# Where eight sums of down-projection weights stand on VectorE, and when their loads begin

## The chip, the cores and the metric

The kernel runs on 1 core of one Trainium2 chip. The metric is the device time of one execution in microseconds (us). Lower is better.

## The reference

One layer of a streaming encoder over 2048 prompt tokens and 8 x 16 sample tokens, width 1024, all in float32. What is computed, cut to the lines that matter here:

```python
qm, km, vm, om, ip, fp, qa, ka, va = split_in(x @ w_in)          # input projection
hm, C1, n1, m1 = mlstm_chunkwise(qm, km, vm, logi, logf, ...)    # matrix memory, 4 heads x 128
ha = swa_prompt(qa, ka, va, attn_sinks)                          # sliding-window attention
mix = jnp.concatenate([hm, ha], axis=-1) @ w_out
h = layer_norm(DEEPNORM_ALPHA * x + mix, ln1_g, ln1_b)
...
u = h @ w_up                                                     # 1024 -> 2 x 2816
c = b_conv + sum(ext[:, j:j + T] * w_conv[j] for j in range(3))  # causal convolution
a, g = jnp.split(c, 2, axis=-1)
f = (jax.nn.silu(g) * a) @ w_down                                # 2816 -> 1024
y = layer_norm(DEEPNORM_ALPHA * h + f, ln2_g, ln2_b)
```

## The kernel before

Every large product is made of three matmuls on halves of float32 numbers: ScalarE rounds an operand to a high half (`split`, L217, or L565 for x), VectorE subtracts to get the low half (L218, L566), and TensorE adds high x high, high x low and low x high. Over that lies a scheme of fast matrix multiplication in which a 2 x 2 block product takes seven products, numbered 1 to 7, instead of eight. It needs sums and differences of blocks of the operands, and a result block is put together from several products by VectorE and ScalarE.

The **input projection** (`i_dense`) runs over 4 blocks b of tokens and, in each, 5 groups g of output columns. Each (b, g) has the seven products. From block 1 on, their order is 1, 7, 6, 2 in group 0; then in every group 5, product 1 of the next group, 3, 4; and in the later groups 6, 7, 2 ahead of that. The last group ends 6, 7, 5, 2, 3, 4. Each product is 24 matmuls of 256 columns (L704). Three PSUM banks A, B, C hold them. After a product `i_after` empties what is due: after product 5 ScalarE copies bank B (L771) and VectorE adds bank C to it (L775 in groups 0 and 1, L777 in the later groups), after 4 VectorE adds bank C to another copy in the same way, after 2 and 3 ScalarE copies bank A and B out (L763). In group 3 the result goes through tanh on ScalarE (L760) and an addition of 1 on VectorE (L761).

Beside this, three chains of smaller work for tokens that are already projected are woven between the matmuls by a planner that works with fixed costs (`Chains.weave`): the matrix memory (among its VectorE steps bst L1150, C L1223, hn L1156, mr L1157 to L1159; ScalarE's mr L1153; TensorE's transposes pht L1176 and products pnum L1211), and the attention. The order of TensorE's instructions is the program's own order; the other engines' orders, and that of SyncE, which issues nearly all DMAs, come from a scheduler that takes the earliest instruction of the program among those it believes ready, by its own estimate of times. Each engine then executes its queue in that fixed order.

The **down projection**, much later, uses the seven products too, and for it needs differences of blocks of its weights. There are 11 pairs of rows of blocks (`NK2`). For each pair, `d_sums(k, step)` does three steps: step 0 loads two 128 x 1024 tiles x and y of weights (L844, L845, 512 KB each), step 1 makes four subtractions of 128 x 512 on VectorE (L850 to L853), step 2 stores x and y to DRAM (L855, L856). All three are called `txy` in the profile. Eight of the pairs are done in blocks 2 and 3 of the input projection, one in each of the groups 0 to 3, the other three in the output projection (`o_block`).

The buffers of the sums are those of the raw x: `xr1` to `xr4`, one for each quarter of a block of x. The next block's quarters are loaded by `x_load` (L537) after product 1 of the last group and turned into halves by `x_steps` beside the products of the last group (L547 is its first difference, of quarters 4 and 2; L550, L553, L557 the others). In the last block, `x_pair` (L892) loads operands of the output projection into the same four buffers. A sum uses `xr1` and `xr3`, so that each sum's loads wait for the store of the sum before.

Of the kernel before, what the change touches and what calls it, by code (L numbers as in the profile page):

```python
# [8 lines left out]
F32 = mybir.dt.float32  # L9
F32R = mybir.dt.float32r  # L10
AF = mybir.ActivationFunctionType
ALU = mybir.AluOpType
AX = mybir.AxisListType

P = 128
D = 1024
# [13 lines left out]
KSCALE = float(np.float32(128.0 ** -0.5))  # L30
# [174 lines left out]
class Prog:  # L205
# [381 lines left out]
    def i_dense(self):  # L587
        nc, a = self.nc, self.a
        nb = len(IBLOCKS)
        last = NG - 1  # L590

        self.next_raw()
        self.x_load(0, 2)
        for _ in range(3):
            self.next_raw()
        self.x_load(0, 4)
        self.single_raw = self.tp.tile([P, KD, P], F32, name="xsr", tag="pth", bufs=2)
        nc.sync.dma_start(self.single_raw, a["xs"])
        self.angles = {}
        self.rope_load(IBLOCKS[0][2], 2)  # L600
        self.rope_load(NPT, 1)
        self.next_split()
        self.x_steps(0, "b12")
        for _ in range(3):
            self.next_split()
        self.x_steps(0, 3)
        self.x_single(1, 2)
        self.x_load(0, 1)
        self.next_raw()
        self.x_load(0, 3)  # L610
        self.x_steps(0, 1)
        self.advance()
        self.x_steps(0, 2, "t3", 7, "t2", 6)
        self.x_single(4)
        self.x_steps(0, "t1", 5, "t4")
        self.sb, self.trans = {}, None

        passages = [{1: ["load"], 7: ["t3", 7], 6: ["t2", 6], 3: [3, "t4"], 4: ["b12", "t1"]},
                    {1: ["load"], 6: ["t3"], 7: [7, "t2"], 5: [6], 3: [3, "t4"], 4: ["b12", "t1"]}]
        sums = 0  # L620
        after = None
        for item in self.items:
            if after:

                after[0] -= 1
                if after[0] == 3:
                    self.logs_of(after[1] - 1)
                if after[0] < 0:
                    self.i_done = after[1]
                    after = None  # L630
            self.chains.hold = item[0] == "t" and item[1] > 0
            if item[0] == "t":
                _, b, ti, e = item
                if ("g", e, 3) not in self.wu:
                    self.advance()
                if b not in self.gates:
                    self.gates[b] = self.tp.tile([P, 5, 8], F32, name="gates", tag="gates", bufs=2)
                ps = self.bank([P, 512], "pg") if ti == 4 else self.ib[ti % 2 * 2]
                yield from self.i_direct(b, ti, e, ps)
                self.i_keys(b, ti, ps)  # L640
                if ti == 1:
                    if b + 1 < nb:
                        self.x_steps(b + 1, 1, 2)
                    else:
                        self.release(4)
                    after = [6, b + 1]
                elif ti == 3 and b or ti == 4:
                    self.release(4)
                    self.x_steps(b, 4)
                    if b:  # L650
                        self.x_steps(b, 5)
                self.advance()
                continue
            _, b, g, s = item
            if item not in self.wu:
                self.advance()
            yield from self.i_product(b, g, s)
            del self.wu[item]
            self.release(2)
            if self.trans and s != 4:  # L660
                self.i_transposes()
            with self.tc.high_priority():
                behind = self.i_after(b, g, s)
            if (b, g, s) == (0, 0, 7):
                self.t_setup()
            if (g, s) == (1, 6):
                self.rope_load(IBLOCKS[b][0], 2)
            if g == last and b + 1 < nb:
                if s == 7:
                    self.rope_load(IBLOCKS[b + 1][2], 2)  # L670
                for x in passages[b > 0].get(s, ()):
                    if x == "load":
                        self.spare = True
                        self.x_load(b + 1, 1, 2, 3, 4)
                    else:
                        self.x_steps(b + 1, x)
            if g == last and b + 1 == nb and s in (7, 5, 2, 3):
                self.x_pair(0, (7, 5, 2, 3).index(s))
            with self.tc.issue_after(behind) if behind and b == 0 else nullcontext():
                self.advance()  # L680

            if b >= nb // 2 and g < last:

                steps = (6, 2, 5) if g == last - 1 else (6, 5, 3)
                if s in steps:
                    self.d_sums(sums, steps.index(s))
                    sums += s == steps[2]
        self.sums = sums
        self.logs_of(nb - 1)
        self.chains.hold = False  # L690
# [64 lines left out]
    def i_out(self, b, g, i, j, src):  # L755

        nc = self.nc
        ev = src if i else self.zev()
        if g == 3:
            nc.scalar.activation(ev, src, AF.Tanh, scale=0.5)  # L760
            nc.vector.tensor_scalar_add(ev, ev, 1.0)  # L761
        elif not i:
            nc.scalar.copy(ev, src)  # L763
        if g == 2:
            self.rope(ev, IBLOCKS[b][2 * j], 2)
        self.i_store(b, g, i, j, ev)

    def i_after(self, b, g, s):
        nc, V = self.nc, self.nc.vector
        A, B, C = self.ib  # L770
        copy = lambda d, x: nc.scalar.activation(d, x, AF.Copy, scale=KSCALE) if g < 2 else nc.scalar.copy(d, x)  # L771

        def add(u):
            if g < 2:
                V.scalar_tensor_tensor(u, C, KSCALE, u, op0=ALU.mult, op1=ALU.add)  # L775
            else:
                V.tensor_add(u, C, u)  # L777
        if s == 1 and g == 0:
            return nc.scalar.copy(B, A).ins
        elif s == 6:  # L780
            self.u2 = self.zev()
            copy(self.u2, B)
        elif s == 2:
            self.i_out(b, g, 0, 0, A)
        elif s == 5:
            u4 = self.zev()
            copy(u4, B)
            add(u4)
            self.i_out(b, g, 1, 1, u4)
        elif s == 4:  # L790
            add(self.u2)
            self.i_out(b, g, 1, 0, self.u2)
            if b == 0:
                self.i_batch(g)
        elif s == 3:
            self.i_out(b, g, 0, 1, B)
            if g + 1 < NG:

                nc.scalar.copy(B, A)
# [40 lines left out]
    def d_sums(self, k, step):  # L840
        nc, V = self.nc, self.nc.vector
        if step == 0:
            self.txy = x, y = [self.xp.tile([P, D], F32, name="txy", tag=f"xr{q}", bufs=1) for q in (1, 3)]
            nc.sync.dma_start(x, self.a["wdn"][k])  # L844
            nc.sync.dma_start(y, self.a["wdn"][NK2 + k])  # L845
            return
        x, y = self.txy
        if step == 1:
            l, r = slice(0, 512), slice(512, D)
            V.tensor_sub(x[:, l], x[:, r], x[:, l])  # L850
            V.tensor_sub(x[:, r], y[:, r], x[:, r])
            V.tensor_sub(y[:, r], y[:, r], x[:, l])
            V.tensor_sub(y[:, l], y[:, l], y[:, r])  # L853
            return
        nc.sync.dma_start(self.zt[0, k], x)  # L855
        nc.sync.dma_start(self.zt[1, k], y)  # L856
# [1329 lines left out]
```

## Time and profile before

| | |
|---|---|
| median of 3 runs | 2314.28 us (2314.28 to 2319.7) |
| the profiled execution's own time | 2316.15 us |
| its span, first to last instruction | 2314.3 us |
| TensorE busy (PE) | 2281.9 us, 99% |
| VectorE busy (DVE) | 1808.1 us, 78% |
| ScalarE busy (ACT) | 1269.0 us, 55% |
| granted TensorE clock, mean | 0.996 |

PE is TensorE's matmuls, PEld its weight loads, DVE VectorE, ACT ScalarE, POOL GpSimd and SPq the queue of SyncE. In a row of a timeline stand start and length in us, engine, line, operation, what it writes and reads, and in brackets how long the engine was idle before and what ended that. Such a releaser is inferred from semaphores. The sums of blocks 2 and 3 lie between 299 and 565 us of the span.

### The profile page before, as it was taken

Reading aid. Unit: us, or ns where it says so; the run is one execution under the profiler, and the core shown is the slowest. Engines: PE = TensorE matmul, PEld = TensorE weight load, DVE = VectorE, ACT = ScalarE, POOL = GpSimd, SP = SyncE. Lnnn points to the kernel's source line nnn. Section 1 sums busy time; section 2 is a strip of 40 time slices with the busy share of each in tenths; the row PEclk is TensorE's granted clock in tenths of the full one; section 3 lists DMA queues with packets and bytes.
Section 4 is the critical chain, followed back from the end, with each engine's and each line's share of the span. In section 5 each row is a group of like instructions: output and inputs, shape, how many; then the busy total and the mean of one; then the engine's idle time right before and its main releaser. Section 6 shows DMA issues by size and latency. Waiting matters only on the chain.

```text
span 2314.3 us, 39788 instructions
## 1 busy us (share of the span) xinstructions
PE 2281.9 (99%) x14293; PEld 2094.9 (91%) x14293; DVE 1808.1 (78%) x3075; ACT 1269.0 (55%) x2377; POOL 279.5 (12%) x509
## 2 busy tenths in 40 slices
PE   8999999999999999999999999999999999999998
PEld 8999989989877778999999999999999978888876
DVE  8777687787688888998788777678766786895987
ACT  5453466776766655555656555555555544444442
POOL 0001000000011212121002000013111200100200
PEclk9999999999999999999999999999999999999999
DMA  7888999999977757888778889978898776756743
GB/s 276 287 308 297 301 309 336 314 310 342 315 269 240 240 201 270 303 319 311 276 289 274 306 304 311 315 264 287 312 294 261 225 282 208 261 175 215 255 157 108
DMA packets 300166, 632.38 MB, mean 273 GB/s; under 512 B 47869, under 2 KB 141121, under 8 KB 299969
## 3 DMA queue, kind: packets, MB, share of 16 engines
q1 hardware_dynamic: 295296, 616.14, 77.9%
q0 software_dynamic: 3520, 10.56, 1.4%
q10 hardware_dynamic: 1152, 3.15, 0.4%
q8 instruction: 113, 1.85, 0.3%
q14 instruction: 85, 0.69, 0.1%
HBM read 458.11 MB, written 171.64 MB: 272 GB/s over the span
## 4 chain that ended last, share of the span: by engine, by line
PE 76%; DVE 5%; DMA 4%; issue 2%; ACT 1%; SPq 0%; POOL 0%; DVEq 0%; ACTq 0%; POOLq 0%
PE dps L1873 19%; PE fup L1873 19%; PE dps L704 7%; PE dps L2083 6%; PE fht L2083 6%; PE fup L2083 6%; PE dps L222 2%; PE dps L224 2%; PE dps L223 2%; PE ppo L1348 1%; PE psc L1303 1%; PE ppt L1342 1%; DVE w L218 1%; PE fht L1697 1%; DMA txy<-wdn 0%
## 5 line engine op out<-in xcount | busy, mean ns | idle before, releaser
L1873 PE MATMUL dps<-hh,uw 128*128 128x384 f32 (+1 forms) x1848 | 478.7, 328 | 2.0 <-DVE u L1904 2.0
L1873 PE MATMUL fup<-hh,uw 128*128 128x384 f32 (+1 forms) x1848 | 478.2, 328 | 1.5 <-ACT ua L1894 1.5
L1873 PEld LDWEIGHTS dps<-hh,uw 128*128 128x128 f32 x1848 | 330.5, 188 | 2.2 <-DVE u L1904 2.2
L1873 PEld LDWEIGHTS fup<-hh,uw 128*128 128x128 f32 x1848 | 330.0, 188 | 2.0 <-ACT ua L1894 1.9
L1930 DVE SCALAR_TENSOR_TENSOR cc<-u,cw,cc 128x768 f32<-128x768 f32 (+1 forms) x264 | 258.1, 978 | 64.9 <-ACT cc L1928 55.5
L1873 PE MATMUL fup<-hl,uw 128*128 128x384 f32 (+1 forms) x924 | 302.5, 327 | 1.7 <-DVE hl L218 1.7
L1873 PE MATMUL dps<-hl,uw 128*128 128x384 f32 (+1 forms) x924 | 302.8, 328 | 0.0
L704 PE MATMUL dps<-w,oh 128*128 128x256 f32 x1344 | 254.3, 284 | 0.7 <-DVE zev L777 0.7
L217 ACT CAST uw<-wraw 128x1024 fp32r<-128x1024 f32 x126 | 123.0, 979 | 223.8 <-PE dps L2083 120.1
L218 DVE TENSOR_TENSOR w<-wraw,w 128x1024 fp32r<-128x1024 f32 (+2 forms) x167 | 189.4, 1141 | 56.1 <-ACT w L217 48.9
L217 ACT CAST w<-wraw 128x1024 fp32r<-128x1024 f32 (+2 forms) x167 | 163.0, 985 | 107.3 <-PE dps L704 38.9
L704 PEld LDWEIGHTS dps<-w,oh 128*128 128x128 f32 x1344 | 210.5, 188 | 11.8 <-issue 8.1
L218 DVE TENSOR_TENSOR uw<-wraw,uw 128x1024 fp32r<-128x1024 f32 x126 | 142.4, 1131 | 65.7 <-ACT uw L217 65.5
L704 PE MATMUL dps<-w,ol 128*128 128x256 f32 x672 | 187.8, 279 | 0.0
L704 PE MATMUL dps<-oh,w 128*128 128x256 f32 x896 | 170.9, 285 | 6.6 <-ACT mr L1153 3.8
L1873 PEld LDWEIGHTS fup<-hl,uw 128*128 128x128 f32 x924 | 173.5, 188 | 2.4 <-DVE hl L218 2.3
L2083 PE MATMUL fup<-uw,fu 128*128 128x512 f32 x726 | 174.2, 396 | 0.6 <-DVE uw L218 0.6
L1873 PEld LDWEIGHTS dps<-hl,uw 128*128 128x128 f32 x924 | 173.8, 188 | 0.0
L2083 PEld LDWEIGHTS fup<-uw,fu 128*128 128x128 f32 x726 | 136.6, 188 | 34.1 <-DVE uw L218 1.1
L2083 PE MATMUL dps<-uw,fu 128*128 128x512 f32 x660 | 165.3, 396 | 1.1 <-DVE uw L218 1.1
L1928 ACT ACTIVATE cc<-u,cw 128x768 f32<-128x768 f32 (+1 forms) x132 | 132.2, 1002 | 57.8 <-DVE u L1910 28.5
L704 PEld LDWEIGHTS dps<-oh,w 128*128 128x128 f32 x896 | 142.2, 191 | 13.1 <-ACT mr L1153 4.1
(318 smaller groups left out, 4567.0 us busy)
## 6 DMA issues: line engine op xcount, KB each, us to landing
uw<-zw SPq DMA_DIRECT2D x176, 512.0 KB, 5.1
zw<-uw SPq DMA_DIRECT2D x88, 512.0 KB, 3.7
w<-zws SPq DMA_DIRECT2D x72, 512.0 KB, 6.2
wv<-wup SPq DMA_DIRECT2D x66, 512.0 KB, 5.0
wraw<-wi SPq DMA_DIRECT2D x65, 512.0 KB, 5.1
wraw<-zt SPq DMA_DIRECT2D x60, 512.0 KB, 4.3
wraw<-wdn SPq DMA_DIRECT2D x45, 512.0 KB, 4.3
wraw<-wo SPq DMA_DIRECT2D x40, 512.0 KB, 4.5
```

The source lines that it names most:

```text
L217: nc.scalar.copy(hi, src)
L218: nc.vector.tensor_sub(lo, src, hi.bitcast(F32))
L222: mm(out, ah, bh, start=start, stop=False)
L223: mm(out, ah, bl, start=False, stop=False)
L224: mm(out, al, bh, start=False, stop=stop)
L704: mm(o, l, r, start=s in (1, 7) and c == k == i == 0, stop=k == 3 and i == 2, skip_group_check=True)
L1303: nc.tensor.matmul(ps[kvh][:, j, :nk], q[rs, j0 + j], k[rs, sel], start=i == 0, stop=i == 2)
L1342: nc.tensor.transpose(pp[:, j * P:(j + 1) * P], scs[j // 2][:, 2 * kvh + j % 2, kt * P:(kt + 1) * P], self.ident)
L1873: mm(ps, l[:, k], r[:, k], start=s in (1, 7) and k == 0 and i == 0, stop=k == 3 and i == 2, skip_group_check=True)
L1928: S.activation(c[:, v], u[:, 2:2 + n], AF.Identity, bias=w[3], scale=w[2])
L1930: V.scalar_tensor_tensor(c[:, v], u[:, i:i + n], w[i], c[:, v], op0=ALU.mult, op1=ALU.add)
L2083: mm(ps, l[:, k, c], r[:, k], start=s in (1, 4, 7) and u == 0 and k == 0 and i == 0, stop=u == nu - 1 and k == n - 1 and i == 2, skip_grou ...
```

## The change

Three things change in the input projection. A sum's load (step 0) moves: the first of a block is begun after product 1 of group 0, the others after product 4 of the group before; until now it was begun after product 6 of its own group. Its subtractions (step 1) are still called at product 5 (at 2 in group 3) and its stores at product 3 (at 5 in group 3), but each VectorE instruction of step 1 gets an ordering edge behind the operation that last emptied a bank, which `i_out` and `i_after` now keep in `self.emptied`: the scheduler may not put it ahead of that one in VectorE's queue. And sums use `xr1` and `xr3`, or `xr2` and `xr4`, in turn, and the next block's quarters are loaded in the order 1, 3, 2, 4.

```diff
@@ i_dense
                     if x == "load":
                         self.spare = True
-                        self.x_load(b + 1, 1, 2, 3, 4)
+                        self.x_load(b + 1, 1, 3, 2, 4)
...
-            if b >= nb // 2 and g < last:
-
-                steps = (6, 2, 5) if g == last - 1 else (6, 5, 3)
-                if s in steps:
-                    self.d_sums(sums, steps.index(s))
-                    sums += s == steps[2]
+            if b >= nb // 2:
+
+                if (g, s) == (0, 1) or s == 4 and g < last - 1:
+                    self.d_sums(sums, 0)
+                    sums += 1
+                elif g < last and s in ((2, 5) if g == last - 1 else (5, 3)):
+                    with self.tc.issue_after(self.emptied):
+                        self.d_sums(sums - 1, 2 if s == 3 or g == last - 1 and s == 5 else 1)
@@ i_out
-            nc.vector.tensor_scalar_add(ev, ev, 1.0)
+            self.emptied = nc.vector.tensor_scalar_add(ev, ev, 1.0).ins
@@ i_after
             if g < 2:
-                V.scalar_tensor_tensor(u, C, KSCALE, u, op0=ALU.mult, op1=ALU.add)
+                self.emptied = V.scalar_tensor_tensor(u, C, KSCALE, u, op0=ALU.mult, op1=ALU.add).ins
             else:
-                V.tensor_add(u, C, u)
+                self.emptied = V.tensor_add(u, C, u).ins
@@ d_sums
         if step == 0:
-            self.txy = x, y = [self.xp.tile([P, D], F32, name="txy", tag=f"xr{q}", bufs=1) for q in (1, 3)]
+            self.txy = x, y = [self.xp.tile([P, D], F32, name="txy", tag=f"xr{q}", bufs=1) for q in ((1, 3), (2, 4))[k % 2]]
```

## The prediction

> **What bounds the kernel now.** I read the page first, then the windows view over the input projection, the waits of TensorE there, and the timelines of VectorE, ScalarE, TensorE and SyncE around each wait.
>
> ```profile
> span 2314.3 us, 39788 instructions
> PE 2281.9 (99%) x14293; PEld 2094.9 (91%) x14293; DVE 1808.1 (78%) x3075; ACT 1269.0 (55%) x2377; POOL 279.5 (12%) x509
> ```
>
> TensorE is busy 99% of the span, idle 2314.3 - 2281.9 = 32.4 us in all. Its instruction order is written out by hand and the change leaves it alone, so the time moves only by TensorE waits that go or come. The change acts on eight of the eleven sums of down-projection weights, between 297 and 565 us. There the windows view (columns: stretch, its length, busy us of PE, PEld, DVE, ACT, POOL with counts, granted clock, DMA share, GB/s) gives
>
> ```profile
> 320.00:360.00 40.00, 36.13 (x294) 34.06 (x294) 30.45 (x86) 29.92 (x80) 3.00 (x6) 0.96 0.97 321
> 360.00:400.00 40.00, 40.00 (x342) 37.48 (x341) 27.29 (x87) 25.10 (x67) 3.84 (x8) 1.00 0.99 343
> 440.00:480.00 40.00, 39.72 (x337) 37.87 (x337) 37.18 (x105) 30.45 (x70) 1.26 (x3) 1.00 0.85 269
> ```
>
> One stretch loses 3.9 us of TensorE and some clock; 360 to 400, with a sum in it, loses nothing. The waits view of TensorE from 290 to 630 us names the losses (us in total, times, longest):
>
> ```profile
> PE dps L704 <- ACT mr L1153: 3.8, 1, 3.8
> PE pht L1176 <- DVE ql L218: 1.0, 1, 1.0
> PE ppo L1348 <- ACT pth L1343: 0.6, 1, 0.6
> PE pnum L1211 <- issue: 0.6, 2, 0.3
> ```
>
> None names a sum, but the timelines lead each of the first three to one. VectorE's:
>
> ```profile
> 325.20 0.69 DVE L850 TENSOR_TENSOR txy<-txy 128x512 f32<-128x512 f32 x1 [3.92 <-DMA txy<-wdn]
> 516.33 0.69 DVE L851 TENSOR_TENSOR txy<-txy 128x512 f32<-128x512 f32 x1 [4.37 <-DMA txy<-wdn]
> 539.60 0.69 DVE L850 TENSOR_TENSOR txy<-txy 128x512 f32<-128x512 f32 x1 [4.22 <-DMA zqk<-zev]
> ```
>
> VectorE works in order. Three times it stood about 4 us at a sum whose weights had not landed (the third is put down to a store of zev, but the operation reads only txy). ScalarE's timeline shows how the first stop reaches TensorE:
>
> ```profile
> 328.63 0.17 ACT L1153 ACTIVATE mr<-pnum 128x2 f32<-128x2 f32 x1 [3.17 <-DVE bst L1150]
> 329.66 0.59 ACT L771 ACTIVATE zev<-dps 128x512 f32<-128x512 f32 x1
> ```
>
> bst (L1150) stood in VectorE's queue behind the sum, ScalarE stood behind bst, and behind that stood the copy L771 that empties the bank TensorE wants.
>
> **The change part by part.** *The early sums go.* The program puts a sum's four subtractions at product 5 of its group, but the schedule pulled them forward into whatever VectorE time it thought free. Now they are tied behind the emptying operation of that product (L775 or L777, and L761 in group 3), and the loads are issued one group sooner, into two pairs of buffers. No operation is added: eight sums of four subtractions, 16 loads and 16 stores stay. A load then has about a group, some 30 us (the first group's L775 follows the copy L771 at 329.66, the next group's is the row of 357.77 below), where before it was wanted ahead of its landing, so I take all three stops as gone. Worth, from TensorE's timeline:
>
> ```profile
> 330.30 0.58 PE L704 MATMUL dps<-oh,w 128*128 128x256 f32 x1 [3.85 <-ACT mr L1153]
> ...
> 330.89 0.63 PE L704 MATMUL dps<-oh,w 128*128 128x256 f32 x2
> 331.32 0.41 PE L704 MATMUL dps<-ol,w 128*128 128x256 f32 x1
> 331.53 0.63 PE L704 MATMUL dps<-oh,w 128*128 128x256 f32 x2
> ...
> 333.24 0.29 PE L704 MATMUL dps<-ol,w 128*128 128x256 f32 x1
> 333.37 0.40 PE L704 MATMUL dps<-oh,w 128*128 128x256 f32 x2
> 333.60 0.28 PE L704 MATMUL dps<-ol,w 128*128 128x256 f32 x1
> 333.72 0.40 PE L704 MATMUL dps<-oh,w 128*128 128x256 f32 x2
> ```
>
> The gap is 3.85 us. After it three matmuls take 0.64 us (330.89 to 331.53), later 0.35 us (333.37 to 333.72): the clock is low until 333.24. Those 2.94 us of work would have taken 2.94 x 0.35/0.64 = 1.6 us, so the slow start cost 1.35 us more. With 1.0 and 0.6 us of the second and third wait, and the two waits of pnum (0.6 us; each wants a product of VectorE that stood behind an early sum), the gain is 3.85 + 1.35 + 1.0 + 0.6 + 0.6 = 7.4 us. What is late next at 330: with the stop gone ScalarE reaches L771 some 4.6 us earlier (3.92 plus the 0.69 of L850), at 325.1, and TensorE wanted the bank at 330.30 - 3.85 = 326.45. So nothing is left of that gap.
>
> [...]
>
> *The block behind the emptying.* Each sum is now some 4 x 0.69 = 2.76 us of VectorE right behind an addition. Queued behind it: the low halves of weights (L218), the chains' bst, C, hn and mr; who waits is the matmul of those weights and the pht transposes. Nearest row: one of the early sums happened to lie around such an addition already,
>
> ```profile
> 357.16 0.69 DVE L852 TENSOR_TENSOR txy<-txy 128x512 f32<-128x512 f32 x1
> 357.77 0.69 DVE L775 SCALAR_TENSOR_TENSOR zev<-dps,zev 128x512 f32<-128x512 f32 x1
> 358.37 0.68 DVE L853 TENSOR_TENSOR txy<-txy 128x512 f32<-128x512 f32 x1
> ```
>
> and TensorE had no wait there: of 320 to 360 us it lost 40 - 36.13 = 3.87 us, which is the one gap of 3.85, and of 360 to 400 none. The far row is the stop at 325.20, where 3.92 us cost 3.85. So a block costs 0 to 2.7 us. I take 0 for seven of the eight, which lie where VectorE is about 70% busy (27.29 of 40 us from 360 to 400), and 0.8 us for the first, which moves from ahead of the stop at 321.3 (325.20 - 3.92) to behind it, where the queue is full. A price below nothing is possible there too, since VectorE is freed of 2.76 us ahead of 321.3.
>
> *The loads of x.* The next block's quarters 2 and 4 used to come early into idle buffers; now those buffers hold sums, and the last sum of block 2 must be stored before they load. Its addition, and the operation that needs both quarters, are here:
>
> ```profile
> 415.62 0.42 DVE L761 TENSOR_SCALAR zev<-zev 128x512 f32<-128x512 f32 x1
> ...
> 432.04 1.22 DVE L547 TENSOR_TENSOR wraw<-xr 128x1024 f32<-128x1024 f32 x1
> 434.32 0.69 DVE L218 TENSOR_TENSOR ql<-pq,qh 128x512 fp32r<-128x512 f32 x1 [1.07 <-ACT qh L217]
> ...
> 437.62 1.23 DVE L218 TENSOR_TENSOR w<-wraw,w 128x1024 fp32r<-128x1024 f32 x1 [2.41 <-ACT w L217]
> ```
>
> Landing times, of txy (loads and stores together), then of xr:
>
> ```profile
> DMA to landing us min/median/max: 3.3/5.2/9.8
> DMA to landing us min/median/max: 3.8/4.5/7.9
> ```
>
> The sum ends at 416.0 + 2.8 = 418.8, or 421.2 if four operations of the chains, of 0.6 us each, come between (an estimate by the 0.69 of L775). With medians quarter 4 is there at 421.2 + 5.2 + 4.5 = 430.9, before 432.04. With the longest it is 421.2 + 17.7 = 438.9, 6.9 us late; VectorE's idle 1.07 + 2.41 behind L547 swallow 3.5, so 0 to 3.4 us, and I take 0.4, near the medians. Quarters 1 and 3 come first in the new order and are free one sum earlier: nothing. In block 3 the next stage's loads wait likewise for the last sum's store, with three products more before they are used: nothing, else a price like that of x. The three later sums stay where they are, one in the other pair of buffers: nothing, as the waits on txy (tile view: us, times)
>
> ```profile
>   DMA txy<-wdn: 11.0, 6
> ```
>
> all lie before 517 us.
>
> SyncE's queue is in order as well:
>
> ```profile
> 505.51 0.47 SPq L856 DMA_DIRECT2D zt<-txy  x1
> 506.09 0.52 SPq L1090 DMA_DIRECT2D qk<-zqk  x1
> 508.90 0.32 SPq L1095 DMA_DIRECT2D og<-zog  x1
> 512.65 0.33 SPq L845 DMA_DIRECT2D txy<-wdn  x1
> ```
>
> A load waiting for its buffer's store issues nothing else, here for 3.4 us. The change keeps such pairs but spreads them over two buffers, and adds two (quarters 2 and 4). [...]
>
> Sum: -7.4 + 0.8 + 0.4 = -6.2 us. The profiled execution took 2316.15 us (span 2314.3), so 2309.95 like it; the median of the runs lies 1.87 us lower, 2308.1. A measurement of this kernel tells about 0.3%, 6.9 us, from no change; the forecast stands just inside.
>
> **The rivals.** *The gain is given back.* Transfers were 97 to 99% of the queues' time from 320 to 400 us at 321 to 343 GB/s; with 5 us less, weights would land late instead. It would leave the two later waits and pnum's, about -2 us: 2312.3. Against it: 360 to 400 us runs at 343 GB/s with no TensorE wait at all, so that pace is sustained.
>
> *Slower: the block holds what TensorE needs.* If what stands behind each addition has no room, each of the eight blocks costs up to 2.7 us: 8 x 2.7 - 7.4 = +14.2 us, 2328.5. It turns the sign from 0.93 us per block. For it: the pace at 325.20, nearly one us of TensorE for each of VectorE's. Against it: 357 to 359 us, and that stops of 4.37 and 4.22 us cost only 1.0 and 0.6.
>
> *x comes late.* The full 3.4 us at L547, a gap that with the low clock adds 1.35: -7.4 + 0.8 + 4.75 = -1.9 us, 2312.4. VectorE is 93% busy from 440 to 480 us and could not catch up. The medians speak against it. That the change does nothing is not open: the waits belong to the early sums, and these must move.
>
> **How the numbers follow.** Forecast 0.58: between -9 and -4, faster by over 6.9 in 0.42 (also when the two unknown costs are nearer nothing and the shift clears small waits), the same in 0.16. Given back 0.10, all the same. The block 0.22: slower 0.19, the same 0.03. x late 0.10: the same 0.09, slower 0.01. Faster 0.42, same 0.38, slower 0.20. The range from 2304 (every wait gone, the two costs nothing and some more waits cleared) to 2322 leaves out most of the slower case, 0.17, and 0.03 below.
>
> **What would show it.** Right: no VectorE wait on txy before 600 us; the gap of 3.85 us and the 0.96 clock gone from 320 to 360; txy operations right behind L775, L777 and L761; the TensorE waits of 290 to 630 us down from about 6 to under 2. Wrong: a VectorE wait on xr at L547, new TensorE waits on L218 or on hn behind the blocks, or SyncE standing before x loads with weight loads behind it.

## The result and the profile after

| kernel | median, us | lowest to highest, runs | ratio to before, 95% interval |
|---|---|---|---|
| before | 2317.11 | 2312.72 to 2323.29, 11 | |
| changed | 2320.90 | 2316.20 to 2326.72, 11 | 1.0020 [1.0010, 1.0029] |

The change makes the kernel 0.2% slower, some 4 us, where 6 us of gain were forecast. It lies within the 0.3% that the prediction called no change, but over 11 runs of each the whole interval lies above 1. The page of the changed kernel's execution (2320.9 us, so the median itself):

```profile
span 2318.8 us, 39768 instructions
PE 2284.8 (99%) x14293; PEld 2094.4 (90%) x14293; DVE 1807.9 (78%) x3075; ACT 1269.4 (55%) x2377; POOL 282.5 (12%) x509
```

No engine has more to do. The stretch that lost 3.87 us of TensorE is mostly mended (1.31 us are left), in the windows view (columns as in the prediction), but another has opened behind it; its row is shown of before, then of after:

```profile
320.00:360.00 40.00, 38.69 (x326) 36.07 (x325) 32.41 (x92) 28.50 (x71) 4.55 (x7) 1.00 0.92 301
360.00:400.00 40.00, 39.93 (x333) 36.26 (x330) 29.75 (x81) 27.05 (x72) 3.23 (x7) 1.00 0.97 341
```

```profile
430.00:445.00 15.00, 15.00 (x121) 12.75 (x120) 9.58 (x14) 11.18 (x24) 2.56 (x4) 1.00 0.98 320
```

```profile
430.00:445.00 15.00, 11.79 (x74) 9.44 (x72) 8.24 (x9) 9.10 (x19) 0.38 (x2) 0.89 0.83 272
```

From 430 to 445 us TensorE, which had not stood at all, now stands 3.21 us, and the granted clock falls to 0.89. The waits view of TensorE, 290 to 630 us, says for what:

```profile
PE dps L706 <- DMA w<-zws: 3.2, 2, 2.3
PE pht L1178 <- ACT hn L1168: 1.2, 2, 0.9
PE dps L706 <- ACT mr L1155: 1.0, 1, 1.0
PE dps L706 <- DVE zev L779: 0.8, 1, 0.8
PE ppo L1350 <- ACT pth L1345: 0.7, 1, 0.7
PE pht L1178 <- DVE ql L218: 0.6, 1, 0.6
```

(Lines of the changed kernel are two higher: L706 is L704 of before, L779 is L777.) Of the old waits the 3.8 on mr has become 1.0; the 3.2 on w<-zws, the halves of weights that TensorE multiplies by, is new, and so are most of the small ones.

TensorE runs the same 14293 matmuls in the same order in every kernel here, so the loss can be placed: the start of each matmul after, less its start before, is taken at the ends of a stretch (by the times of before), and the table shows by how much it grew there, in us. It holds gaps and slow clock alike. The kernels are those of the experiments below, and each row is one profiled execution. Ahead of 290 us these kernels differ by -2.3 to +3.0 us from before, so only stretches are compared.

| kernel | 290 to 325 | 325 to 360 | 360 to 430 | 430 to 445 | 445 to 480 | 480 to 560 | 560 to 640 | sum |
|---|---|---|---|---|---|---|---|---|
| changed | +0.3 | -3.4 | +2.1 | +5.1 | -0.5 | -1.9 | +3.3 | +5.0 |
| edge_only | +0.4 | -3.5 | +2.2 | +5.5 | -0.2 | -1.6 | +2.2 | +5.1 |
| small_sums | +0.3 | -3.0 | 0.0 | +6.7 | 0.0 | -2.4 | +0.5 | +2.3 |
| early_last | +1.4 | -3.4 | +2.7 | +5.4 | -0.5 | -1.4 | +1.4 | +5.5 |
| swap_pool | +0.2 | -3.4 | +2.2 | +1.0 | +0.8 | -2.2 | +0.5 | -0.8 |
| halves | +0.3 | -2.3 | +0.4 | +0.5 | +0.4 | -1.2 | +2.5 | +0.6 |
| spread | +0.3 | -3.4 | +0.4 | +4.1 | +0.7 | -2.4 | +2.5 | +2.1 |
| small_both | +1.5 | -3.0 | 0.0 | +0.6 | +0.3 | -2.1 | 0.0 | -2.6 |
| mixed | -0.1 | -3.5 | +0.5 | +0.8 | +0.3 | -1.1 | +1.2 | -1.9 |

The first row is the whole answer: a gain of 3.4 + 1.9 + 0.5 = 5.8 us is there, and 5.1 us at one place and 2.1 + 3.3 = 5.4 us in small pieces are paid for it. The experiments separate these.

**Where the 5.1 us come from.** The two waits in TensorE's timeline, with the matmuls behind them:

```profile
431.44 0.36 PE L706 MATMUL dps<-w,oh 128*128 128x256 f32 x1 [0.88 <-DMA w<-zws]
431.63 0.28 PE L706 MATMUL dps<-w,ol 128*128 128x256 f32 x1
434.24 0.79 PE L706 MATMUL dps<-w,oh 128*128 128x256 f32 x2 [2.32 <-DMA w<-zws]
...
435.47 0.41 PE L706 MATMUL dps<-w,ol 128*128 128x256 f32 x1
...
436.11 0.41 PE L706 MATMUL dps<-w,ol 128*128 128x256 f32 x1
...
437.51 0.40 PE L706 MATMUL dps<-w,oh 128*128 128x256 f32 x2
...
437.87 0.40 PE L706 MATMUL dps<-w,oh 128*128 128x256 f32 x2
```

It waits first for the high half of the weights of product 7 of block 2's last group, then for the low half. The windows view has a granted clock of 0.50 from 434.24 to 437.39 us and of 1.00 from 437.51 to 440: three matmuls take 0.64 us (435.47 to 436.11), then 0.36 us (437.51 to 437.87). The 15 matmuls from 434.24 to 437.51 so took 3.27 us instead of some 1.8 (an estimate, 15 at 0.36 us for three): 3.2 us are gaps, some 1.5 slow clock, and the remaining 0.4 lie at the few matmuls around the two gaps. Why the weights are late stands in SyncE's timeline, of before and then of after:

```profile
419.93 0.80 SPq L753 DMA_DIRECT2D zog<-zev  x2
420.77 0.46 SPq L537 DMA_DIRECT2D xr<-xq  x1
421.34 1.16 SPq L483 DMA_DIRECT2D w<-zws  x2
425.26 0.79 SPq L753 DMA_DIRECT2D zog<-zev  x2
426.15 0.96 SPq L483 DMA_DIRECT2D w<-zws  x2
```

```profile
418.25 0.48 SPq L857 DMA_DIRECT2D zt<-txy  x1
418.77 0.46 SPq L858 DMA_DIRECT2D zt<-txy  x1
419.29 0.82 SPq L537 DMA_DIRECT2D xr<-xq  x1
422.47 0.80 SPq L755 DMA_DIRECT2D zog<-zev  x2
423.67 1.27 SPq L537 DMA_DIRECT2D xr<-xq  x2
425.04 0.37 SPq L483 DMA_DIRECT2D w<-zws  x1
428.25 1.15 SPq L755 DMA_DIRECT2D zog<-zev  x2
429.50 1.35 SPq L483 DMA_DIRECT2D w<-zws  x3
```

Before, the two halves went out from 421.34 on, ahead of the next two stores of zog. After, these stores (422.47) and three loads of x (the last two of them, at 423.67, need the last sum's stores) stand ahead of the first half, at 425.04. The second half is behind two stores of zog more, for which SyncE stood 2.8 us until VectorE had their data: 429.50, 7 us later than before.

### The profile page after: what moved, and what is told of

Read it like the earlier page. It is cut to its first block, busy times and chain, and to the rows that moved or that the text cites. A ratio compares the mean times of both kernels' runs of the same rounds, so it can differ in the third digit from the quotient of the medians.

```text
span 2318.8 us, 39768 instructions
## 1 busy us (share of the span) xinstructions
PE 2284.8 (99%) x14293; PEld 2094.4 (90%) x14293; DVE 1807.9 (78%) x3075; ACT 1269.4 (55%) x2377; POOL 282.5 (12%) x509
## 3 DMA queue, kind: packets, MB, share of 16 engines
q10 hardware_dynamic: 1152, 3.15, 0.4%
## 5 line engine op out<-in xcount | busy, mean ns | idle before, releaser
L706 PE MATMUL dps<-w,oh 128*128 128x256 f32 x1344 | 256.5, 285 | 4.0 <-DMA w<-zws 3.2
L217 ACT CAST uw<-wraw 128x1024 fp32r<-128x1024 f32 x126 | 123.0, 979 | 224.1 <-PE dps L2085 120.1
L218 DVE TENSOR_TENSOR w<-wraw,w 128x1024 fp32r<-128x1024 f32 (+2 forms) x167 | 189.2, 1141 | 53.1 <-ACT w L217 45.7
L706 PEld LDWEIGHTS dps<-w,oh 128*128 128x128 f32 x1344 | 211.9, 189 | 15.5 <-issue 9.2
L217 ACT CAST w<-wraw 128x1024 fp32r<-128x1024 f32 (+2 forms) x167 | 163.0, 984 | 110.6 <-PE dps L706 34.3
L218 DVE TENSOR_TENSOR uw<-wraw,uw 128x1024 fp32r<-128x1024 f32 x126 | 142.2, 1129 | 65.6 <-ACT uw L217 65.5
L706 PE MATMUL dps<-w,ol 128*128 128x256 f32 x672 | 188.4, 280 | 0.0
L706 PE MATMUL dps<-oh,w 128*128 128x256 f32 x896 | 168.7, 283 | 3.7 <-DVE w L218 1.3
L2085 PEld LDWEIGHTS dps<-uw,fu 128*128 128x128 f32 x660 | 123.9, 188 | 31.4 <-DVE uw L218 1.5
```

The lines of the kernel that those rows point to most:

```text
L217: nc.scalar.copy(hi, src)
L218: nc.vector.tensor_sub(lo, src, hi.bitcast(F32))
L706: mm(o, l, r, start=s in (1, 7) and c == k == i == 0, stop=k == 3 and i == 2, skip_group_check=True)
L2085: mm(ps, l[:, k, c], r[:, k], start=s in (1, 4, 7) and u == 0 and k == 0 and i == 0, stop=u == nu - 1 and k == n - 1 and i == 2, skip_grou ...
```

## Experiments

Each kernel is the changed one with the edit shown, timed against before on the same chip; a median is followed by that ratio and its interval, and losses by stretch are in the table above or stand with the run.

### Parts of the change

**One pair of buffers** (`one_pair`).

```diff
-                        self.x_load(b + 1, 1, 3, 2, 4)
+                        self.x_load(b + 1, 1, 2, 3, 4)
...
-            self.txy = x, y = [... for q in ((1, 3), (2, 4))[k % 2]]
+            self.txy = x, y = [... for q in (1, 3)]
```

> The changed kernel, but every sum uses xr1 and xr3 again and the quarters of x load in the order 1, 2, 3, 4; the ordering edge and the earlier loads stay. Theory Q (SyncE's queue: with the edge the last sum of block 2 is stored late, and its stores and the x loads behind them push the loads of the kept weights for the products of the last group behind the zog stores): here two x loads still wait for that store, and one weight load still stands ahead of and one behind a pair of zog stores, so the TensorE waits on w<-zws near 432 us stay (3.2 us and the low clock), and the time is that of the changed kernel, 2319 to 2322, +0.1 to +0.2% on before. Theory X (quarters 2 and 4 late for L547, as my rival said): they come early again, the waits near 432 us go, and the time is 2311 to 2314.

Measured: 2325.91 us, 1.0038 [1.0025, 1.0051], slower than the change. Quarters 2 and 4 are free early again, and the waits on w<-zws are there all the same, 4.4 us in four, 3.2 of them near 432 us (5.0 us lost from 430 to 445). So it is not that quarters 2 and 4 come late for L547. What makes this run slower than the change lies mostly elsewhere: 5.5 us are lost from 640 to 700 us, with a wait of 3.85 us of ppt for pth.

**The edge alone** (`edge_only`): besides the edit above, the loads begin after product 6 again.

```diff
-                if (g, s) == (0, 1) or s == 4 and g < last - 1:
+                if s == 6 and g < last:
```

> The kernel before with the ordering edge alone: loads after product 6 of a sum's own group, one pair of buffers. SyncE's queue then has one load of w<-zws ahead of the stores of zog at 420 us and its partner behind them, as in the changed kernel. Theory Q (the partner held behind those stores): TensorE still waits 2 to 3.5 us on w<-zws near 432 us. Theory B (a block of four subtractions right behind an emptying makes small waits): those on hn, zev and ql stay too, some 3 us in all. Both: 2318 to 2323 us, and no VectorE stop of over 2 us on txy, since the edge alone moves the subtractions late enough. Rival: the earlier loads are what ended the stop, and VectorE still stands 2 to 4 us at 325 us.

Measured: 2324.41 us, 1.0033 [1.0021, 1.0045]. All of the loss and all of the gain from 290 to 640 us are here (+5.1). VectorE waits once on txy, 0.5 us. The edge both ends the stops and makes the losses; 3.9 us more are lost at 640 to 700 us, in the same wait of ppt for pth (3.87 us; 1.65 before, 1.50 in the changed kernel). Why one pair of buffers with the edge lengthens this wait was not tried.

**No edge** (`no_edge`): two pairs and early loads stay.

```diff
-                    with self.tc.issue_after(self.emptied):
+                    with nullcontext():
```

> The changed kernel without the ordering edge: earlier loads and two pairs alone. If the edge is what brings the w<-zws waits (theory Q), these are gone here, and since the loads have longer to land, the VectorE waits on txy are small too: 2311 to 2315, below before. If the two pairs bring them (theory X), they stay: 2319 to 2323. If the edge was what removed the VectorE waits on txy, they are back at three places and the 3.85 us gap with them: 2317 to 2320.

Measured: 2320.37 us, 1.0015 [1.0002, 1.0027]. The scheduler pulls the subtractions forward again and VectorE stops at them, in its waits view

```profile
DVE txy L853 <- DMA txy<-wdn: 7.2, 3, 4.3
DVE txy L852 <- DMA txy<-wdn: 5.8, 2, 3.0
```

13.0 us (11.0 before the change, or 15.2 with the stop put down to a store of zev), and TensorE waits elsewhere for it (5.4 us lost from 360 to 430). Earlier loads and two pairs without the edge bring nothing.

### SyncE's queue

**Quarters 2 and 4 from GpSimd's queue** (`x_pool`).

```diff
-            self.nc.sync.dma_start(r, self.a["xq"][b]...)
+            (self.nc.gpsimd if b == 3 and q in (2, 4) else self.nc.sync).dma_start(r, self.a["xq"][b]...)
```

> The changed kernel, but the loads of quarters 2 and 4 of the last block's x are issued from GpSimd's queue, so SyncE does not stand or spend issue time at them; they still wait for the last sum's stores. Theory Q: the weight loads stand ahead of the zog stores again, the w<-zws waits near 432 us go, 5 to 7 us under the changed kernel, 2313 to 2316. Theory X: x is as late as now or later, L547 and the waits stay, 2320 to 2324. Theory D (the transfers themselves are too many at once): unchanged, 2319 to 2322.

Measured: 2320.68 us, 1.0012 [1.0001, 1.0023]. The loss from 430 to 445 us falls from 5.1 to 0.9 us, but now x is late. VectorE's waits view has

```profile
DVE wraw L547 <- DMA xr<-xq: 5.5, 1, 5.5
```

and 445 to 480 us costs 2.1 instead of -0.5. In the changed kernel L547 came without any wait, at 434.19, and both quarters it needs had landed by 429.86. Here they were issued at 426.61 and 427.84 and landed at 434.71 and 437.22. The DMA views from 420 to 436 us (size of one, median us from issue to landing), of the changed kernel and then of this run, show that the weights' loads went from 6.3 to 9.0 us and those of x from 4.3 to 8.7, here with four loads of weights issued from 426.02 to 427.81, beside the two of x:

```profile
w<-zws SPq DMA_DIRECT2D x6, 512.0 KB, 6.3
xr<-xq SPq DMA_DIRECT2D x3, 512.0 KB, 4.3
```

```profile
w<-zws SPq DMA_DIRECT2D x4, 512.0 KB, 9.0
xr<-xq POOLq DMA_DIRECT2D x2, 512.0 KB, 8.7
```

So theory D holds in part: taking the weights out of the wait behind x does not shorten what has to be moved.

**Weight loads ahead of all else** (`kept_first`).

```diff
+            with self.tc.high_priority():
                 for i, t in enumerate((hi, lo)):
                     self.nc.sync.dma_start(t..., self.zws[u[2]]...)
```

> The changed kernel, but the loads of kept weight halves (w<-zws) are given high priority in the schedule, so that SyncE issues them ahead of x loads and stores. Theory Q: no TensorE wait on w<-zws, 2312 to 2316. Theory X: quarters 2 and 4 of x are still behind the last sum's stores, time as the changed kernel or more, 2320 to 2325. Theory D: waits on w<-zws become waits on something else of the same size, 2319 to 2322.

Measured: 2322.81 us, 1.0026 [1.0014, 1.0039]. No wait on w<-zws is left (0.0 from 430 to 445 us), but VectorE waits 2.1 us for x at L547, and TensorE 1.3, 1.2 and 2.7 us at 459, 464 and 481 us: 445 to 480 us costs 7.1 us. The weights' lateness is their place in the queue; moving them put x in that place.

**The last sum earlier** (`early_last`): the pairs in the other order, so that quarters 2 and 4 are free a sum sooner, and the last sum tied to the addition after product 4 of the group before.

```diff
-                        self.x_load(b + 1, 1, 3, 2, 4)
+                        self.x_load(b + 1, 2, 4, 1, 3)
...
+                if s == 4:
+                    self.emptied4 = self.emptied
...
-                    with self.tc.issue_after(self.emptied):
+                    with self.tc.issue_after(self.emptied4 if g == last - 1 else self.emptied):
...
-            self.txy = ... ((1, 3), (2, 4))[k % 2]]
+            self.txy = ... ((2, 4), (1, 3))[k % 2]]
```

> The changed kernel with the pairs in the other order (quarters 2 and 4 first) and the last sum of a block put behind the addition after product 4 of the group before, about two products sooner; all loads on SyncE. The stores of the last sum are then done before SyncE comes to the loads of x, but in SyncE's order three loads of x still stand ahead of one load of w<-zws, and its partner behind the stores of zog. Theory Q, as place in the queue: TensorE still waits 2.5 to 3.3 us on w<-zws near 432 us, and the time is 2319 to 2322. Theory Q2, that the wait for the last sum's stores is what holds the weights: those waits are under 1 us, and the time is 2316 to 2318.

Measured: 2320.12 us, 1.0021 [1.0010, 1.0033]. In SyncE's timeline the sum's stores no longer stand around the loads of x, yet

```profile
423.88 1.06 SPq L537 DMA_DIRECT2D xr<-xq  x2
427.04 0.80 SPq L757 DMA_DIRECT2D zog<-zev  x2
427.89 1.17 SPq L537 DMA_DIRECT2D xr<-xq  x2
429.17 0.41 SPq L483 DMA_DIRECT2D w<-zws  x1
433.22 0.80 SPq L757 DMA_DIRECT2D zog<-zev  x2
434.11 1.84 SPq L483 DMA_DIRECT2D w<-zws  x3
```

has the same pattern, one half ahead of the stores of zog and one behind, and TensorE waits 3.4 us. So it is not the wait for the sum's stores that holds the weights, but their place behind the loads of x and the stores of zog.

**Other pairs, quarters 1 and 3 from GpSimd's queue** (`swap_pool`): the two edits of the pairs in `early_last`, and `x_pool`'s with quarters (1, 3).

> The changed kernel with the pairs in the other order (quarters 2 and 4 first), so that the last sum of block 2 holds quarters 1 and 3, and these two quarters loaded from GpSimd's queue. Quarters 2 and 4, which L547 needs first, are then free a sum sooner, and no load of weights stands behind a wait for the last sum's store. Theory Q: TensorE's waits on w<-zws near 432 us fall from 3.2 to under 0.5 us, L547 does not wait, and the time falls by 3 to 5 us against the changed kernel, to 2316 to 2318. Theory D (the transfers of these stretches are too many, whoever issues them): a wait of the same size turns up at another transfer, and the time stays at 2320 to 2322.

Measured: 2317.93 us, 1.0003 [0.9993, 1.0014], 3 us below the change by the medians. The wait on w<-zws is 0.8 us, no VectorE wait on x, and the loss from 430 to 445 us 1.0. The held weight loads are one half of the price. In this run the loss from 560 to 640 us, too, is 0.5 instead of 3.3, though every sum stands whole as in the change; why was not tried.

### VectorE's blocks

**Subtractions of 64 columns** (`small_sums`), which leaves out seven eighths of each difference and keeps every load, store and edge.

```diff
-            V.tensor_sub(x[:, l], x[:, r], x[:, l])
... (four of 512 columns)
+            for t in (x, y):
+                V.tensor_sub(t[:, :64], t[:, 512:576], t[:, :64])
+                V.tensor_sub(t[:, 512:576], t[:, 512:576], t[:, :64])
```

> The changed kernel with subtractions of 64 columns instead of 512: it leaves out seven eighths of each difference, in all eleven sums, and keeps every load, store and edge. VectorE is freed of about 11 x 4 x 0.5 = 22 us. SyncE's order still has one load of w<-zws behind the stores of zog. Theory Q: the waits on w<-zws near 432 us stay (2 to 3.2 us). Theory B: the rest of the first gap (1.0 us at 325), the waits on hn, zev, ql and pth (0.9, 0.75, 0.6, 0.66) go, 3 us in all, and the time is 2317 to 2319. If VectorE's blocks cost nothing, the time is that of the changed kernel; if they are all of it, 2314 and below.

Measured: 2317.32 us, 1.0008 [0.9999, 1.0017]. TensorE's waits, 290 to 640 us:

```profile
PE dps L706 <- DMA w<-zws: 3.8, 2, 2.6
PE dps L706 <- ACT dps L801: 1.1, 1, 1.1
PE dps L706 <- ACT mr L1154: 1.0, 1, 1.0
```

The waits on hn, zev, ql and pth are gone, and 360 to 430 and 560 to 640 us cost 0.0 and 0.5 us instead of 2.1 and 3.3. The 3.8 on w<-zws and the 1.0 on mr stay, against what was expected of mr: the rest of the first gap doesn't come from the length of the blocks. The run takes work off VectorE altogether, so it doesn't tell a block's place from its length.

**Both away** (`small_both`): `swap_pool` with 64 columns.

> The same as swap_pool with subtractions of 64 columns instead of 512: it leaves out seven eighths of each difference in all eleven sums. Both suspected costs are gone, the held weight load and VectorE's blocks, and what the change took away (the first gap, the waits at 518 and 550 us) stays away. If these two are the whole cost: 3.5 to 5 us below the kernel before, 2311 to 2312.5. If a third cost is there: the time of the kernel before or above, and a wait shows it.

Measured: 2312.37 us, 0.9982 [0.9973, 0.9991], 4.2 us below before. With both costs removed a gain stands alone, 2.6 us from 290 to 640 us in the profiled execution, and 1.5 us of the 5.8 are lost there to a wait for gates at 297 us. No third price of the size of the two is left.

**Two halves** (`halves`): `swap_pool` with two subtractions behind the addition after product 5 and two behind that after product 4 (in group 3 after products 2 and 5); the new last argument of `d_sums` picks the half.

```diff
+                first, second = (2, 5) if g == last - 1 else (5, 4)
+                if g < last and s in (first, second):
+                    with self.tc.issue_after(self.emptied):
+                        self.d_sums(sums - 1, 1, 1 if s == first else 2)
+                    if s == second:
+                        self.d_sums(sums - 1, 2)
```

> The same as swap_pool, and each sum's four subtractions in two halves, two behind the addition after product 5 and two behind that after product 4 (in group 3 after products 2 and 5). Theory B: what stands behind an addition waits for 1.4 us instead of 2.8, so the waits on hn at 402 us, zev at 570 and ql and pth at 621 to 624 fall by half or go, and the time is 1 to 2 us below that of swap_pool. Rival: these waits come from where the scheduler puts the steps of the chains, not from a block's length, and the time is that of swap_pool within 0.5 us.

Measured: 2317.18 us, 1.0000 [0.9990, 1.0010]. 360 to 430 us costs 0.4 instead of 2.2, but 325 to 360 gains 1.1 less and 560 to 640 costs 2.0 more than in `swap_pool`. The time is 0.8 us below that of `swap_pool`, between the 1 to 2 us of theory B and the 0.5 of the rival: halves move the cost more than they remove it.

**One by one** (`spread`): the four at products 5, 1, 3 and 4.

> The same as swap_pool (pairs in the other order, quarters 1 and 3 of the last block from GpSimd's queue), and each sum's four subtractions one by one, at products 5, 1, 3 and 4 (in group 3 two at product 2 and two at 5). Theory B (what stands behind an addition waits as long as the block is): the waits on hn and gates of swap_pool fall further than with halves, and the time is 1 to 2 us below that of halves, at 2315 to 2316.5. Rival: halves took all that can be had, and the time is the same within 0.7 us or more, since each subtraction still delays some step of a chain.

Measured: 2318.62 us, 1.0005 [0.9993, 1.0016]; not below `halves`. 360 to 430 us costs 0.4 here too, but a wait of 2.28 us on w<-zws is back at 432.04. It is for the second half, issued at 423.03 and wanted 6.7 us later, as in `halves`, which waited 0.24 us. The first half (422.51) landed at 429.02, the second only at 431.99. Here one of the loads of x from GpSimd's queue went out ahead of both halves, at 422.25; in `halves` both went out behind them. Whether this is the 2.3 us was not tried.

**Halves for two sums only** (`mixed`): the sums of groups 2 and 3 of block 2 in halves, the other six whole.

```diff
+                two = b == nb // 2 and g in (2, 3)
+                first, second = (2, 5) if g == last - 1 else (5, 4 if two else 3)
+                if g < last and s in (first, second):
+                    if two or s == first:
+                        with self.tc.issue_after(self.emptied):
+                            self.d_sums(sums - 1, 1, (1 if s == first else 2) if two else 0)
+                    if s == second:
+                        self.d_sums(sums - 1, 2)
```

> The same as swap_pool, with the subtractions in two halves only for the sums of groups 2 and 3 of block 2 (behind the additions after products 5 and 4, or 2 and 5), and whole for the other six. Theory B by place: block 2's loss at 400 to 430 us falls from 1.85 us to about 0.1 as with halves, the first gap stays won (-3.4 us at 325 to 360), and block 3 stays as in swap_pool (-1.7 us in all from 480 to 640). Against swap_pool 2 to 3 us less, 2313.5 to 2315, and below the kernel before by 1 to 3 us. Rival: a block's price belongs to no place, each new order of VectorE makes small waits somewhere else, and the time is that of halves and swap_pool within 1 us.

Measured: 2313.69 us, 0.9982 [0.9973, 0.9992], faster than both kernels and inside what was expected. The profiled execution:

```profile
span 2310.3 us, 39787 instructions
PE 2282.9 (99%) x14293; PEld 2094.6 (91%) x14293; DVE 1807.6 (78%) x3075; ACT 1268.3 (55%) x2377; POOL 283.4 (12%) x511
```

Block 2 keeps the first gap's 3.5 us and pays 0.5 from 360 to 430, as expected by place. In block 3, where the sums stand whole as in `swap_pool`, 480 to 640 us came out 1.8 us dearer than there; that part of the expectation failed. From 290 to 640 us the sum is -1.9 us, 1.0 below `swap_pool`; 2.3 us more were gained in this execution behind 640 us, at waits of about 1 us that other kernels show or not. Whether these belong to the edit was not tried.

**The same with the weight loads first** (`mixed_kept`): `mixed` and the edit of `kept_first`.

> The same as mixed with the loads of w<-zws issued ahead of all else in SyncE's order, as in kept_first. Theory Q (place in the queue): no wait on w<-zws from 425 to 445 us, where mixed still has 0.2 to 2.3 us; quarter 4 is loaded from a place further back, and VectorE may wait up to 2 us at L547. Rival D (transfer time): a wait of the same size stays, at the weights or elsewhere. By the losses of kept_first ahead of 290 us (2 us) the time is no better than that of mixed: 2314 to 2318.

Measured: 2313.67 us, 0.9980 [0.9969, 0.9990], the same as `mixed`. SyncE's timeline:

```profile
421.61 0.80 SPq L761 DMA_DIRECT2D zog<-zev  x2
422.50 3.43 SPq L484 DMA_DIRECT2D w<-zws  x4
426.64 0.81 SPq L761 DMA_DIRECT2D zog<-zev  x2
...
429.06 0.57 SPq L538 DMA_DIRECT2D xr<-xq  x1
```

No wait on w<-zws is left from 430 to 445 us (0.0 lost), and L547's counterpart waits 0.4 us for x. What was left near 432 us was place in the queue. It pays elsewhere: 5.2 us between 200 and 290 us in this execution, ahead of the sums.

## Why the prediction was wrong

**The stops go: right.** VectorE has no wait on txy from 290 to 640 us, and the waits at 518 and 550 us and one of pnum's two are gone: 480 to 560 us gained 1.9 us of the 2.2 forecast for these waits. The other wait of pnum, at 319 us, stayed (0.25 us), so no early sum was behind that one.

**"Nothing is left of that gap": wrong by about 1 us.** The gap of 3.85 us is one of 0.99, and with the clock it gave 3.4 us instead of 5.2. ScalarE's timeline shows it:

```profile
323.76 0.17 ACT L1155 ACTIVATE mr<-pnum 128x2 f32<-128x2 f32 x1 [1.20 <-DVE bst L1152]
323.84 1.05 ACT L217 CAST w<-wraw 128x1024 fp32r<-128x1024 f32 x1
324.79 0.59 ACT L773 ACTIVATE zev<-dps 128x512 f32<-128x512 f32 x1
```

The prediction took the whole 3.92 + 0.69 us off ScalarE's lateness. But mr still waits 1.20 us for bst, and L773 comes at 324.79 in an execution that runs 2 us ahead there, 1.7 us later than forecast. `small_sums` and `small_both` keep the 1.0 us, so the length of the sums has nothing to do with this rest. The prediction left out that L218, ahead of that bst in VectorE's queue, needs a high half from ScalarE (L217). In the changed kernel L217 ran at 319.87 for 1.03 us and L218 began at 320.93, after 0.76 us of waiting. Seen from TensorE that is 1.5 us later than the stop's end alone would put it, most of the 1.7.

**The loads of x and SyncE's queue: 0.4 us taken, 5.1 measured.** This step decided. It looked for the price at L547, where x is used, and there was none to see (L547 at 434.19 without a wait). It was at the loads of weights behind x in SyncE's queue. The prediction named that queue, wrote an upper 3.4 us beside its own 0.4 and chose the smaller. What held the second half in the changed kernel was the wait of 2.8 us for the stores of zog ahead of it: SyncE issued nothing from 425.41 to 428.25 us. The prediction looked at the waits of x only; it did not ask what order the scheduler would give the loads of weights once those of x came later, and so missed the stores of zog. Its rival of the late x came to 4.75 us with the slow clock, close to 5.1, but by luck: that price was to be paid by VectorE at L547, and L547 did not wait.

**The block behind the emptying: 0.8 us taken, between 2.1 and 5.4 measured.** "Nothing for seven of the eight" rested on VectorE being about 70% busy and on one sum of before that happened to stand at such a place without a wait. Between 360 and 430 us and between 560 and 640 us that was not so:

```profile
401.99 1.21 PE L1178 MATMUL pht<-ident,hn 128*128 128x128 f32 x4 [0.88 <-ACT hn L1168]
```

```profile
569.93 0.38 PE L706 MATMUL dps<-w,oh 128*128 128x256 f32 x1 [0.75 <-DVE zev L779]
```

With 64 columns both waits are gone. The 2.1 us from 360 to 430 are the blocks': they are 2.1 to 2.7 in every run of the table that has the last sums of block 2 whole (`swap_pool` too), and 0.5 or less where they are halved, spread or narrow. The first of the two waits shows how they arise. The block before it began its four subtractions between 385.17 and 388.44, with other steps between them, and VectorE then had no idle time until behind 400 us, so that its delay passed on to the steps behind, mr and hn among them. For the 3.3 us from 560 to 640 it is not shown: with whole blocks `swap_pool` pays 0.5 there. Were all 5.4 us the blocks', they would be 0.7 each, below the 0.93 at which the rival of the blocks would have turned the sign alone. Neither that rival nor the late x is the cause by itself; the forecast treated as alternatives two costs that came together.

**The sum.** -3.4 - 1.9 - 0.5 + 0.3 + 5.4 + 5.1 = +5.0 us in the profiled executions; the ratio of the runs gives +4.6. The forecast time also started from a median of three runs, 2314.28 us; that of eleven is 2317.11, so 2.8 us of its distance from 2320.90 have nothing to do with the change. TensorE's waits from 290 to 630 us, which were to fall below 2 us, add up to 8.7. What the prediction had named as signs of a failure, a new TensorE wait on L218 or hn behind the blocks, and SyncE at the x loads with weight loads behind it, both came; the VectorE wait on xr did not.

## What to carry to other kernels

When a load is made to wait longer, price it where the next loads in the same queue are used, not only where its own data is: list what the queue issues behind it, in which order the scheduler will place them, and how much time each has in hand. A stretch in which VectorE was about 70% busy was not free here for blocks of 2.8 us (2.1 us lost from 360 to 430 us); ask of each place which steps stand behind it until the engine is next idle, and who waits for them. And add up costs of different queues before treating them as rivals, since here each alone (swap_pool, small_sums) brought the kernel back to where it was, and only both removed (small_both, mixed) made the gain visible.

## What the runs showed of the hardware

Behind two waits of 0.88 and 2.32 us with 0.5 us of matmuls between them the granted clock was 0.50 for 3.15 us (434.24 to 437.39), as it was from 330.30 to 333.24 us behind the single gap of 3.85 us in the kernel before. Behind the single wait of 2.28 us in `spread` (up to 432.04) three matmuls took 0.63 to 0.64 us from 432.60 to 435.79, then 0.36. Behind the single waits of 1.34 and 1.20 us in `kept_first` (up to 459.04 and 463.64) three matmuls of 264 columns took 0.36 to 0.37 us, as ahead of them. In the changed kernel the slow clock cost some 1.5 us (the estimate above) on top of the 3.2 of the waits, which the waits view doesn't show.
